# The last LayerNorm of a decoder layer: bias terms by adding DMAs, 1/sigma by ScalarE

## The chip, the cores and the metric

The kernel runs on one core of a Trainium2 chip. The core has five engines with an instruction stream each: TensorE (PE; its weight loads are listed as PEld), VectorE (DVE), ScalarE (ACT), GpSimd (POOL) and SyncE (SP), which in this kernel only issues DMAs. Data move between DRAM and the core's own memory (SBUF) by 16 DMA engines, and matmuls write into banks of PSUM. An engine executes its stream in order: an instruction that waits holds everything behind it on that engine. A DMA that is issued and waits for something holds its issuing engine in the same way.

The metric is the device time of one execution in microseconds, as the median of several runs. Lower is better.

## What is computed

One decoder layer over 4096 tokens of width 1024, in float32. Two mixers with a common input projection are followed by one output projection and a LayerNorm. What matters here is the end of it, from the reference:

```python
shift, scale, gate = jnp.split(mod, 3, axis=-1)
...
y = jnp.concatenate([y_a, y_b], axis=-1) @ w_out + b_out
x = layer_norm(DEEPNORM_ALPHA * x + gate[:, None, :] * y) * ln_post_g + ln_post_b
```

`gate` has one value per column (there is one sequence), so the gated bias `gate * b_out` is one row of 1024 values that is added to every token. DEEPNORM_ALPHA is 2 to the power 0.25. The LayerNorm needs the mean and the variance of each token, and 1/sigma = (variance + 1e-5) to the power -0.5.

## The kernel before

**Phases.** Phase 1 and phase 2 compute the input projection and what follows from it and leave their results in DRAM, by blocks of 512 tokens. The depthwise convolution and its LayerNorm run on VectorE beside them. Phase 3 takes the eight blocks of 512 tokens one after the other; it is the part that the change is in.

**A block of phase 3.** `prep(sb)` loads the convolution's results (`t`) and mixer A's results (`ya`), and splits each into a high part and a rest: matrices are multiplied as three products of such parts, so that TensorE's reduced precision loses little. The high part is a copy by ScalarE (L184), the rest a subtraction on VectorE (L185, in `split`). `pw_stage(sb)` does the pointwise product of the convolution branch: four results of 12 matmuls each, multiplied with `z` on VectorE, and split again into `yb0` to `yb3`. Then `out_tile(sb, t)` does four tiles of 128 tokens. Tiles are counted through all blocks, i = 4 sb + t, from 0 to 31.

**An output tile.** It loads 128 rows of x into a buffer `r` (L638; three buffers in turn) and forms ALPHA * x + gbo on VectorE (L639). `gbo` is the gated bias, the same row on all 128 partitions; it is made once in phase 1. TensorE multiplies the eight parts of y, 128 columns each (`ya` first, then `yb`), with the gated weights into two PSUM banks `po` of 512 columns: 48 matmuls (L647). There are four such banks, so two tiles can be under way. VectorE adds each bank to its half of `r` and sums the rows as it goes (L665, the eviction), and turns the sums into minus the mean (`osm`, L667). ScalarE squares `r` with that bias into a throwaway tile and sums it (L670, `oss`). VectorE turns this into variance plus epsilon (`ove`, L672), GpSimd raises it to -0.5 (`ors`, 1/sigma, L676). Two operations on VectorE finish the tile: (r - mean) * g (L678) and r * 1/sigma + b (L679), where `g_bc` and `b_bc` hold the rows of g and b on all partitions. SP stores `r` to `out` (L680). The very last tile, i = 31, computes its two halves one after the other and takes mean and variance from VectorE's own statistics operations.

**What else runs there.** Two of the eight blocks of the convolution are computed late, by VectorE, between the tiles (`late_unit`), and so is their LayerNorm (`conv_ln`). For that TensorE transposes the results into the bank `s2b`, ScalarE sums them, and GpSimd raises the variances to -0.5 (`ccs`, L263). TensorE then transposes the statistics (`ccp`).

**What sets the order.** The program is written as one sequence. A scheduler that simulates the engines with its own costs puts each engine's instructions into an order when the kernel is built; it follows data dependencies, free buffers and the dependencies that `after` adds by hand. SP issues nearly all loads and stores of phase 3 from one stream.

Of the kernel before, what the change touches and what calls it, by code (L numbers as in the profile page):

```python
# [9 lines left out]
F32 = mybir.dt.float32  # L10
# [3 lines left out]
ALU = mybir.AluOpType  # L14
# [3 lines left out]
P = 128  # L18
S = 4096
D = 1024  # L20
DH = 512
T = 512
NSB = S // T
TT = T // P
# [11 lines left out]
ALPHA = 2.0 ** 0.25  # L36
# [3 lines left out]
def tile_layer(ctx, tc, x, x_t, w_in_t, c, w_ada, b_ada, w_in, b_in, w_pool, b_pool, ls_pool, w_dw, b_dw,  # L40
# [20 lines left out]

# [1 line left out]
    ident = cst.tile([P, P], F32, name="ident")  # L63
# [28 lines left out]

# [1 line left out]
    crow = s2.tile([P, P], F32, tag="cto", bufs=2, name="crow", padded_shape=[P, T])  # L94
# [37 lines left out]

# [1 line left out]
    def mod_gate(acc):  # L134
# [48 lines left out]
    def split(hi, lo, src, eng=nc.vector):  # L183
        nc.scalar.copy(hi, src)  # L184
        eng.tensor_tensor(lo, src, hi.bitcast(F32), op=ALU.subtract)  # L185

# [48 lines left out]
    cD = [dr.tile([4 * TT, P], F32, name=f"cD{sb}") for sb in range(NSB)]  # L235
    rD = [dr.tile([8, P], F32, name=f"rD{sb}") for sb in range(NSB)]
    uD = [dr.tile([P, D], F32, name=f"uD{g}") for g in range(MC)]

# [3 lines left out]
    gate_bc = cst.tile([P, D], F32, tag="gate", name="gate_bc")  # L242
    gbo = cst.tile([P, D], F32, name="gbo")
    bpl = cst.tile([P, MC], F32, name="bpl")
    bu = cst.tile([P, MC], F32, name="bu")
    W = {}

# [1 line left out]
    ph_ctx = ExitStack()  # L249
# [116 lines left out]

    # modulation
    xt_next = [load_x(t) for t in range(TT)]
# [22 lines left out]
    for sb in range(NSB):  # L391
# [30 lines left out]
        if sb == 1:  # L422
            mod_gate(gbo)
            gb = wraw("gb")
            nc.sync.dma_start(gb, b_ada[2 * D : 3 * D].partition_broadcast(P))
            for h in range(2):
                sl = slice(h * 512, (h + 1) * 512)
                gp = tp_bank(f"gp{h}")
                nc.tensor.matmul(gp, ones, gbo[:, sl], start=True, stop=True)
                nc.vector.tensor_tensor(gate_bc[:, sl], gp, gb[:, sl], op=ALU.add)  # L430
            nc.sync.dma_start(gbo, b_out.partition_broadcast(P))
            nc.vector.tensor_tensor(gbo, gbo, gate_bc, op=ALU.mult)
    ph_ctx.close()
    lt = pool("lt", reuse_waits="tile")

# [1 line left out]
    ph_ctx = ExitStack()  # L437
# [52 lines left out]

# [1 line left out]
    def conv(m, s0, n, v, tmp, a):  # L492
# [94 lines left out]

# [1 line left out]
    ph = pool("ph3", reuse_waits="tile")  # L589
# [27 lines left out]
    def pw_stage(sb, vs, ys):  # L617
        for m in range(MC):
# [14 lines left out]
            ys.append(h2)  # L633

    def out_tile(sb, t, ys):
        i = sb * TT + t
        r = ph.tile([P, D], F32, tag="r", bufs=3, name=f"r{i}")
        nc.sync.dma_start(r, tok(xv, i))  # L638
        xg = nc.vector.scalar_tensor_tensor(r, r, ALPHA, gbo, op0=ALU.mult, op1=ALU.add)  # L639
        po = [acc_bank(f"po{i}_{h}") for h in range(2)]  # L640
        fin = i == NSB * TT - 1
        for hs in ((0,), (1,)) if fin else ((0, 1),):
            for k in range(KT):
                yh, yl = ys[k][:, 0, t * P : (t + 1) * P], ys[k][:, 1, t * P : (t + 1) * P]
                for lhs, wi, last in ((yh, 0, False), (yh, 1, False), (yl, 0, k == KT - 1)):
                    for h in hs:
                        mm = nc.tensor.matmul(po[h], lhs, Wo[k][wi][:, h * 512 : (h + 1) * 512],  # L647
                                              start=(k == 0 and wi == 0 and lhs is yh), stop=last)
                if k == 0 and hs[0] == 0:
                    after(xg, mm)  # L650
        halves = [slice(0, 512), slice(512, 1024)]
        if fin:
            bs = st.tile([P, 2, 6], F32, tag="xbs", bufs=4, name="obs")
            for h, sl in enumerate(halves):
                nc.vector.tensor_tensor(r[:, sl], po[h], r[:, sl], op=ALU.add)
                nc.vector.bn_stats(bs[:, h, :], r[:, sl])
# [5 lines left out]
        else:  # L662
            sm = st.tile([P, 3], F32, tag="osm", bufs=4, name=f"osm{i}")
            for h, sl in enumerate(halves):
                nc.vector.scalar_tensor_tensor(r[:, sl], po[h], 1.0, r[:, sl], op0=ALU.mult, op1=ALU.add,  # L665
                                               accum_out=sm[:, h : h + 1])
# [8 lines left out]
        rs = st.tile([P, 1], F32, tag="ors", bufs=4, name=f"ors{i}")  # L675
        nc.gpsimd.tensor_tensor(rs, ve, mhalf[:, 0:1], op=ALU.pow)  # L676
        for sl in halves:
            nc.vector.scalar_tensor_tensor(r[:, sl], r[:, sl], mean, g_bc[:, sl], op0=sub, op1=ALU.mult)  # L678
            nc.vector.scalar_tensor_tensor(r[:, sl], r[:, sl], rs, b_bc[:, sl], op0=ALU.mult, op1=ALU.add)  # L679
            nc.sync.dma_start(tok(ov, i)[:, sl], r[:, sl])  # L680
# [3 lines left out]
    for k in range(KT):  # L684
# [3 lines left out]
        hi, lo = wslot(f"wo{k}")  # L688
        split(hi, lo, raw)
        Wo.append((hi, lo))  # L690
    g_bc = cst.tile([P, D], F32, tag="gate", name="g_bc")
    nc.sync.dma_start(g_bc, ln_post_g.partition_broadcast(P))
    b_bc = ph.tile([P, D], F32, name="b_bc", bufs=1)
    nc.sync.dma_start(b_bc, ln_post_b.partition_broadcast(P))
# [45 lines left out]
```

## Time and profile before

| | |
|---|---|
| median of 3 runs | 1400.14 us (1399.49 to 1400.76) |
| span of the profiled execution | 1404.7 us (its time is not listed separately) |
| instructions in it | 17113 |
| ScalarE busy | 431.7 us (31%), 764 instructions |
| GpSimd busy | 167.2 us (12%), 203 instructions |
| DMA, mean over the span | 174 GB/s, 243.82 MB |
| queue of the DMAs that GpSimd issues | 33.56 MB, 7.2% of 16 engines' span |

The page has six parts: busy time by engine, the span in 40 slices (a digit is the busy share in tenths), the DMA queues, the chain of work that ended last, the costliest groups of instructions, and the DMA issues. A group's line names the source line, the engine, the operation, output and inputs by the program's names, the count, and then its busy time with the mean of one, and the idle time ahead of them with what ended most of it. The slices of 35.1 us show which phase a time falls in: phase 1 runs up to some 500 us, phase 2 from there to about 950 us, and the 32 output tiles lie between 957 and 1396 us, with a few microseconds at the end for the last tile's normalisation and store.

All transfers of GpSimd's queue are in phase 2 here (`x2r`, L326, which loads stored x-transposes): 64 of 512 KB. In phase 3 GpSimd has only the powers.

### The profile page before, as it was taken

The page shows a single profiled execution, that of the slowest core. Times are in us where ns is not written, and L with a number is a line of the kernel's source. Part 1 is how long each engine was busy: PE and PEld are TensorE (multiplying, and loading weights), DVE is VectorE, ACT ScalarE, POOL GpSimd, SP SyncE. Part 2 cuts the span into 40 slices and gives each one's busy share as a digit, 9 for nine tenths or more (in the row PEclk, how much of TensorE's full clock was granted, in tenths as well). Part 3 has the DMA queues.
Part 4 walks back from the last instruction along what each step waited for, and adds up shares of the span by engine and source line. Part 5 has one row for each costly group of instructions (what it writes and reads, how often), then busy time and mean ns, then how long its engine had stood idle before and what let it go on. Part 6 is the DMA issues. An engine that isn't in the chain of part 4 may idle for free.

```text
span 1404.7 us, 17113 instructions
## 1 busy us (share of the span) xinstructions
PE 1357.8 (97%) x6044; PEld 1118.6 (80%) x6044; DVE 1193.9 (85%) x2318; ACT 431.7 (31%) x764; POOL 167.2 (12%) x203
## 2 busy tenths in 40 slices
PE   3989999999999999999999999989999999999997
PEld 2878888888788888888888888778888888888886
DVE  7669999983479999899898699979897899998654
ACT  3535335344531322311114111434134131322310
POOL 4310000000100011110011110410111101001111
PEclk9999999999999999999999999989999999999999
DMA  9778776567474563361440741455444443433511
GB/s 313 235 279 312 257 276 241 173 255 242 162 253 151 174 210 124 111 202 42 161 166 31 239 136 61 136 183 173 161 173 138 155 158 122 157 128 122 191 62 75
DMA packets 119496, 243.82 MB, mean 174 GB/s; under 512 B 15026, under 2 KB 52722, under 8 KB 119410
## 3 DMA queue, kind: packets, MB, share of 16 engines
q1 hardware_dynamic: 109952, 209.07, 43.4%
q0 software_dynamic: 9216, 33.56, 7.2%
q8 instruction: 47, 0.77, 0.2%
q14 instruction: 39, 0.32, 0.1%
q10 hardware_dynamic: 242, 0.10, 0.0%
HBM read 156.65 MB, written 86.04 MB: 173 GB/s over the span
## 4 chain that ended last, share of the span: by engine, by line
PE 87%; DVE 4%; DMA 4%; ACT 2%; POOL 1%; issue 1%; SPq 1%; DVEq 0%; ACTq 0%
PE po L647 25%; PE p L335 6%; PE p L334 6%; PE p L333 6%; PE p2u L333 4%; PE p2u L334 4%; PE p2u L335 4%; PE p2z L333 4%; PE p2z L335 4%; PE p2z L334 4%; PE pw L623 2%; PE pw L625 2%; PE pw L624 2%; PE p2b L333 2%; PE p2b L335 2%; PE p2b L334 2%
## 5 line engine op out<-in xcount | busy, mean ns | idle before, releaser
L510 DVE SCALAR_TENSOR_TENSOR cx<-cv,wdw,cx 128x513 f32<-128x513 f32 (+1 forms) x240 | 144.6, 611 | 0.7
L510 DVE SCALAR_TENSOR_TENSOR ca<-cx,wsum,ca 128x256 f32<-128x256 f32 (+1 forms) x240 | 143.1, 608 | 0.1
L510 DVE SCALAR_TENSOR_TENSOR ca<-cv,wdw,ca 128x256 f32<-128x256 f32 (+1 forms) x224 | 133.5, 608 | 0.0
L676 POOL TENSOR_TENSOR ors<-ove,mhalf 128x1 f32<-128x1 f32 x32 | 46.3, 1447 | 409.3 <-DVE ove L672 400.9
L326 POOL DMA_DIRECT2D x2r<-xD x64 | 34.5, 540 | 402.7 <-PE p2b L335 276.4
L670 ACT ACTIVATE ojk<-r,osm 128x1024 bf16<-128x1024 f32 x31 | 35.6, 1149 | 148.3 <-DVE osm L667 148.3
L665 DVE SCALAR_TENSOR_TENSOR r<-po,r 128x512 f32<-128x512 f32 x62 | 40.8, 685 | 23.3 <-PE po L647 23.3
L510 DVE SCALAR_TENSOR_TENSOR lx<-lv,wdw,lx 128x257 f32<-128x257 f32 x120 | 57.2, 477 | 0.0
L510 DVE SCALAR_TENSOR_TENSOR la<-lx,wsum,la 128x256 f32<-128x256 f32 x120 | 57.0, 475 | 0.0
L451 ACT ACTIVATE sz<-p2z,cols 128x512 f32<-128x512 f32 x32 | 22.0, 687 | 108.0 <-PE p2z L335 108.0
L263 POOL TENSOR_TENSOR xcs<-smx,mhalf 128x1 f32<-128x1 f32 x28 | 19.2, 688 | 290.7 <-DVE smx L262 263.9
L297 ACT ACTIVATE x<-xk,shc 128x512 fp32r<-128x512 f32 x56 | 38.5, 721 | 47.5 <-DVE xk L288 46.1
L510 DVE SCALAR_TENSOR_TENSOR la<-lv,wdw,la 128x256 f32<-128x256 f32 x112 | 52.9, 475 | 0.0
L286 DVE TENSOR_TENSOR xk<-xk,xbc 128x1024 f32<-128x1024 f32 x28 | 34.0, 1220 | 16.7 <-DMA xk<-in_x_t_dram 16.5
L263 POOL TENSOR_TENSOR ccs<-smc,mhalf 128x1 f32<-128x1 f32 x32 | 37.2, 1169 | 91.9 <-DVE smc L262 91.2
L298 DVE SCALAR_TENSOR_TENSOR x<-xk,shc,x 128x512 fp32r<-128x512 f32 x56 | 40.4, 744 | 8.1 <-ACT x L297 8.1
L458 ACT ACTIVATE u<-p2u,bu 128x512 f32<-128x512 f32 x32 | 22.0, 689 | 75.6 <-PE p2u L335 75.6
L679 DVE SCALAR_TENSOR_TENSOR r<-r,ors,b_bc 128x1024 f32<-128x1024 f32 (+1 forms) x33 | 41.0, 1246 | 3.2 <-POOL ors L676 3.1
L647 PE MATMUL po<-wo0h,ya 128*128 128x512 f32 x128 | 41.2, 392 | 0.0
L647 PE MATMUL po<-wo1h,ya 128*128 128x512 f32 x128 | 41.1, 390 | 0.0
L259 ACT ACTIVATE x<-x 128x1024 f32<-128x1024 f32 x28 | 29.6, 1059 | 35.7 <-DMA x<-in_x_dram 35.2
L639 DVE SCALAR_TENSOR_TENSOR r<-r,gbo 128x1024 f32<-128x1024 f32 x32 | 38.9, 1217 | 1.8 <-DMA r<-in_x_dram 1.8
(356 smaller groups left out, 4137.8 us busy)
## 6 DMA issues: line engine op xcount, KB each, us to landing
x2r<-xD POOLq DMA_DIRECT2D x64, 512.0 KB, 7.8
xD<-x SPq DMA_DIRECT2D x56, 512.0 KB, 6.9
x<-in_x_dram SPq DMA_DIRECT2D x32, 512.0 KB, 7.9
r<-in_x_dram SPq DMA_DIRECT2D x32, 512.0 KB, 4.4
out_dram<-r SPq DMA_DIRECT2D x31, 512.0 KB, 2.6
xk<-in_x_t_dram SPq DMA_DIRECT2D x28, 512.0 KB, 6.5
wa<-in_w_ada_dram SPq DMA_DIRECT2D x32, 256.0 KB, 4.8
wr<-in_w_in_dram SPq DMA_DIRECT2D x16, 512.0 KB, 6.5
```

The costliest lines, as they stand in the source:

```text
L263: nc.gpsimd.tensor_tensor(rstd, sm[:, 2:3], mhalf[:, 0:1], op=ALU.pow)
L297: nc.scalar.activation(h2[:, 0, :], z, AF.Identity, bias=shc[:, k : k + 1])
L298: nc.vector.scalar_tensor_tensor(h2[:, 1, :], z, shc[:, k : k + 1], h2[:, 0, :].bitcast(F32), op0=ALU.add, op1=ALU.subtract)
L333: nc.tensor.matmul(ps, wh, X[0], start=first, stop=False)
L334: nc.tensor.matmul(ps, wh, X[1], start=False, stop=False)
L335: nc.tensor.matmul(ps, wl, X[0], start=False, stop=last)
L510: nc.vector.scalar_tensor_tensor(dst, src, wt, dst, op0=ALU.mult, op1=ALU.add)
L639: xg = nc.vector.scalar_tensor_tensor(r, r, ALPHA, gbo, op0=ALU.mult, op1=ALU.add)
L647: mm = nc.tensor.matmul(po[h], lhs, Wo[k][wi][:, h * 512 : (h + 1) * 512], start=(k == 0 and wi == 0 and lhs is yh), stop=last)
L665: nc.vector.scalar_tensor_tensor(r[:, sl], po[h], 1.0, r[:, sl], op0=ALU.mult, op1=ALU.add, accum_out=sm[:, h : h + 1])
L676: nc.gpsimd.tensor_tensor(rs, ve, mhalf[:, 0:1], op=ALU.pow)
L679: nc.vector.scalar_tensor_tensor(r[:, sl], r[:, sl], rs, b_bc[:, sl], op0=ALU.mult, op1=ALU.add)
```

## The change

It changes five things, all for the 31 tiles ahead of the last but where it says otherwise.

1. **The gated bias.** `gbo` becomes b_out * gate / ALPHA (one operation on VectorE as before), and its first row is stored to a small DRAM buffer `gD`. The SBUF buffer is then reused for `b_bc`, which is loaded in phase 1 now.
2. **Loading r.** SP loads x into `r` as before, and a second DMA, issued by GpSimd, adds the row `gD` to all 128 partitions of `r` in place. L639 is gone. This holds for all 32 tiles. The eviction computes r * ALPHA + po (the same operation on VectorE with other operands); in the last tile it takes the place of an addition. There are four buffers of `r` in the place of three.
3. **The final bias.** Ahead of each load of `r`, SP stores `b_bc` to the rows of `out` that belong to the tile (the fill). It waits for a marked operation of VectorE: the multiplication by g of the tile three before, or a split of the weights for the first ones.
4. **1/sigma.** ScalarE multiplies `r` by it (L685 of the changed kernel), in the place of L679 on VectorE, which also added b.
5. **The store.** GpSimd issues a DMA that adds `r` to the filled rows of `out`. The last tile keeps its two operations on VectorE and its plain stores.

```diff
+    gD = dr.tile([1, D], F32, name="gD")
...
-    gbo = cst.tile([P, D], F32, name="gbo")
+    gbo = cst.tile([P, D], F32, tag="gbo", name="gbo")
...
-            nc.vector.tensor_tensor(gbo, gbo, gate_bc, op=ALU.mult)
+            nc.vector.scalar_tensor_tensor(gbo, gbo, 1.0 / ALPHA, gate_bc, op0=ALU.mult, op1=ALU.mult)
+            nc.sync.dma_start(gD, gbo[0:1, :])
...
+    def load_r(i):
+        r = ph.tile([P, D], F32, tag="r", bufs=4, name=f"r{i}")
+        if i < NSB * TT - 1:
+            after(nc.sync.dma_start(tok(ov, i), b_bc), marks[-min(len(marks), 3)], True)
+        nc.sync.dma_start(r, tok(xv, i))
+        nc.gpsimd.dma_start(r, gD[0].partition_broadcast(P), accum_op=ALU.add)
+        return r
...
-        r = ph.tile([P, D], F32, tag="r", bufs=3, name=f"r{i}")
-        nc.sync.dma_start(r, tok(xv, i))
-        xg = nc.vector.scalar_tensor_tensor(r, r, ALPHA, gbo, op0=ALU.mult, op1=ALU.add)
+        r = load_r(i)
...
-                nc.vector.scalar_tensor_tensor(r[:, sl], po[h], 1.0, r[:, sl], op0=ALU.mult, op1=ALU.add,
+                nc.vector.scalar_tensor_tensor(r[:, sl], r[:, sl], ALPHA, po[h], op0=ALU.mult, op1=ALU.add,
                                                accum_out=sm[:, h : h + 1])
...
+        if not fin:
+            marks.append(nc.vector.scalar_tensor_tensor(r, r, mean, g_bc, op0=sub, op1=ALU.mult))
+            nc.scalar.mul(r, r, rs)
+            nc.gpsimd.dma_start(tok(ov, i), r, accum_op=ALU.add)
+            return
...
-        split(hi, lo, raw)
+        marks = [split(hi, lo, raw)]
...
-    b_bc = ph.tile([P, D], F32, name="b_bc", bufs=1)
+    b_bc = cst.tile([P, D], F32, tag="gbo", name="b_bc")
```

The change also moves instructions on the engines. Line numbers in the rows below are those of each kernel's own text; a number behind the last underscore of a name only tells buffers apart.

GpSimd, in the block of tiles 20 to 23. Before, five powers of tiles 19 to 23 stand one behind the other:

```order
L676 TENSOR_TENSOR ors19_10106<-ove19_10104,mhalf_82 128x1
L676 TENSOR_TENSOR ors20_10342<-ove20_10340,mhalf_82 128x1
L676 TENSOR_TENSOR ors21_10409<-ove21_10407,mhalf_82 128x1
L676 TENSOR_TENSOR ors22_10476<-ove22_10474,mhalf_82 128x1
L676 TENSOR_TENSOR ors23_10543<-ove23_10541,mhalf_82 128x1
```

In the changed kernel the powers are at L682, the adding stores at L686 and the adding loads at L642:

```order
L682 TENSOR_TENSOR ors20_10365<-ove20_10363,mhalf_82 128x1
L686 DMA out_0_dram<-r20_10302 128x1024
L642 DMA r24_10808<-gD_317 128x1024
L682 TENSOR_TENSOR ors21_10433<-ove21_10431,mhalf_82 128x1
L686 DMA out_0_dram<-r21_10370 128x1024
L642 DMA r25_10876<-gD_317 128x1024
L682 TENSOR_TENSOR ors22_10501<-ove22_10499,mhalf_82 128x1
L686 DMA out_0_dram<-r22_10438 128x1024
L642 DMA r26_10944<-gD_317 128x1024
```

Between the powers of two tiles there are now the adding store of the one and the adding load of the tile four later, whose buffer `r` is the one that the store reads.

ScalarE, at the end of the block of tiles 16 to 19. `ojk18` and `ojk19` are the squares of the last two tiles, `yb5_0` to `yb5_3` the high parts of the pointwise product that tiles 20 to 23 need, `vp6` those of a product one block later. Before:

```order
L670 ACTIVATE ojk18_10034,oss18_10035<-r18_9977,osm18_10030 128x1024
L184 CAST yb5_0_10184<-z5_0_10181 128x512
L184 CAST yb5_1_10201<-z5_0_10181 128x512
L670 ACTIVATE ojk19_10101,oss19_10102<-r19_10044,osm19_10097 128x1024
L184 CAST vp6_2_10255<-t6_2_10252 128x512
L184 CAST vp6_3_10261<-t6_3_10258 128x512
L184 CAST yb5_2_10220<-z5_2_10217 128x512
L184 CAST yb5_3_10237<-z5_2_10217 128x512
```

After, with the scalings at L685:

```order
L676 ACTIVATE ojk18_10055,oss18_10056<-r18_9997,osm18_10051 128x1024
L685 ACTIVATE r18_9997<-r18_9997,ors18_10060 128x1024
L676 ACTIVATE ojk19_10123,oss19_10124<-r19_10065,osm19_10119 128x1024
L184 CAST yb5_0_10206<-z5_0_10203 128x512
L685 ACTIVATE r19_10065<-r19_10065,ors19_10128 128x1024
L184 CAST yb5_1_10223<-z5_0_10203 128x512
L184 CAST vp6_2_10277<-t6_2_10274 128x512
L184 CAST yb5_2_10242<-z5_2_10239 128x512
L184 CAST vp6_3_10283<-t6_3_10280 128x512
L184 CAST yb5_3_10259<-z5_2_10239 128x512
```

The scaling of tile 18 stands between the two squares, and that of tile 19 between the copies for `yb5_0` and `yb5_1`.

SP, near the end. Before, loads of `r` (L638) and stores to `out` (L680) alternate:

```order
L638 DMA r28_11122<-in_x_dram 128x1024
L680 DMA out_0_dram<-r26_10916 128x1024
L638 DMA r29_11189<-in_x_dram 128x1024
L680 DMA out_0_dram<-r27_10983 128x1024
L638 DMA r30_11256<-in_x_dram 128x1024
L680 DMA out_0_dram<-r28_11122 128x1024
L638 DMA r31_11323<-in_x_dram 128x1024
```

After, `t7` are the loads of `prep` for the last block (L605), L640 the fills from `b_bc`, L641 the loads of `r`:

```order
L605 DMA t7_1_10774<-tD1_7_252 128x512
L545 DMA tD3_7_268<-la7_2_10133 128x512
L640 DMA out_0_dram<-b_bc_7919 128x1024
L605 DMA t7_2_10780<-tD2_7_260 128x512
L605 DMA t7_3_10786<-tD3_7_268 128x512
L641 DMA r28_11152<-in_x_dram 128x1024
L640 DMA out_0_dram<-b_bc_7919 128x1024
L641 DMA r29_11220<-in_x_dram 128x1024
L640 DMA out_0_dram<-b_bc_7919 128x1024
L641 DMA r30_11288<-in_x_dram 128x1024
```

The stores of `r` are gone from SP's stream, and in their place each load of `r` has a fill ahead of it; loads of the next block's `t` stand behind the fill that waits for VectorE.

More of the change, by code (lines that the diff above doesn't have):

```diff
@@ L184, in split @@
         nc.scalar.copy(hi, src)
-        eng.tensor_tensor(lo, src, hi.bitcast(F32), op=ALU.subtract)
+        return eng.tensor_tensor(lo, src, hi.bitcast(F32), op=ALU.subtract)
     def wslot(name):
@@ L646, in out_tile @@
                     for h in hs:
-                        mm = nc.tensor.matmul(po[h], lhs, Wo[k][wi][:, h * 512 : (h + 1) * 512],
+                        nc.tensor.matmul(po[h], lhs, Wo[k][wi][:, h * 512 : (h + 1) * 512],
                                               start=(k == 0 and wi == 0 and lhs is yh), stop=last)
-                if k == 0 and hs[0] == 0:
-                    after(xg, mm)
         halves = [slice(0, 512), slice(512, 1024)]
@@ L654, in out_tile @@
             for h, sl in enumerate(halves):
-                nc.vector.tensor_tensor(r[:, sl], po[h], r[:, sl], op=ALU.add)
+                nc.vector.scalar_tensor_tensor(r[:, sl], r[:, sl], ALPHA, po[h], op0=ALU.mult, op1=ALU.add)
                 nc.vector.bn_stats(bs[:, h, :], r[:, sl])
```

## The prediction

> **What bounds the kernel now.** The page's first two parts come first: which engine is busy, and whether it is so everywhere.
>
> ```profile
> span 1404.7 us, 17113 instructions
> PE 1357.8 (97%) x6044; PEld 1118.6 (80%) x6044; DVE 1193.9 (85%) x2318; ACT 431.7 (31%) x764; POOL 167.2 (12%) x203
> PE   3989999999999999999999999989999999999997
> ```
>
> TensorE is busy for 97% of the span, and every slice but the first, the last and two others is full. VectorE's 85% is high, but it is no bound unless TensorE waits for it. So the next view is the busy time by stretch, cut where the stages change (columns: stretch, its length, busy time and count of PE, PEld, DVE, ACT, POOL, then PE's clock, DMA share, GB/s).
>
> ```profile
> 900.00:957.00 57.00, 49.75 (x211) 40.56 (x210) 49.17 (x91) 21.09 (x36) 12.66 (x3) 0.91 0.50 162
> 957.00:1396.00 439.00, 439.00 (x1945) 361.75 (x1944) 369.81 (x742) 119.81 (x212) 49.78 (x39) 1.00 0.41 141
> 1396.00:1405.00 9.00, 0.87 (x4) 0.38 (x2) 4.39 (x8) 0.00 (x0) 0.92 (x1) 0.75 0.15 58
> ```
>
> The changed stage, the 32 output tiles, is the middle row. There TensorE is busy 439.00 of 439.00 us at full clock: work taken from any other engine in it has nothing to shorten. The stage can only stay, or grow a wait. The list of TensorE's waits has one large entry outside the start-up:
>
> ```profile
> PE ccp L77 <- POOL ccs L263: 7.3, 1, 7.3
> ```
>
> **The change part by part.** The profile's own time is not listed beside its span; the span is 1404.7 us, 4.6 above the median 1400.14 of the runs. I work with differences inside the span and add them to that median.
>
> What goes from VectorE:
>
> ```profile
> L679 DVE SCALAR_TENSOR_TENSOR r<-r,ors,b_bc 128x1024 f32<-128x1024 f32 (+1 forms) x33 | 41.0, 1246 | 3.2 <-POOL ors L676 3.1
> L639 DVE SCALAR_TENSOR_TENSOR r<-r,gbo 128x1024 f32<-128x1024 f32 x32 | 38.9, 1217 | 1.8 <-DMA r<-in_x_dram 1.8
> L670 ACT ACTIVATE ojk<-r,osm 128x1024 bf16<-128x1024 f32 x31 | 35.6, 1149 | 148.3 <-DVE osm L667 148.3
> L676 POOL TENSOR_TENSOR ors<-ove,mhalf 128x1 f32<-128x1 f32 x32 | 46.3, 1447 | 409.3 <-DVE ove L672 400.9
> L326 POOL DMA_DIRECT2D x2r<-xD x64 | 34.5, 540 | 402.7 <-PE p2b L335 276.4
> L185 DVE TENSOR_TENSOR yb<-z,yb 128x512 fp32r<-128x512 f32 x32 | 21.9, 684 | 4.4 <-ACT yb L184 4.4
> ```
>
> All 32 of L639 (38.9) and 31 of the 33 of L679 (31 x 1.27 = 39.4) leave VectorE: 78 us, 2.5 a tile. By the stage's row TensorE gains none of it. The eviction (now r times ALPHA plus po) keeps its form and its 0.69 us. ScalarE gets 31 scalings of 128x1024; the nearest row is L670 at 1.15 us, 36 us in all, on an engine that is busy 119.81 of 439 us. The changed product for gbo, its store to gD and the earlier load of b_bc lie in phase 1, alone and beside full slices: nothing, while TensorE stays full there. If they moved work there, at most one 1.27 us operation is late.
>
> What is added is 31 stores of b_bc, 32 adding loads and 31 adding stores of 512 KB, the adding ones issued by GpSimd. For the price of a transfer, from issue to landing, I read the DMA issues of the stretch 1100 to 1390, and of the whole run, and the queue's bytes and share:
>
> ```profile
> r<-in_x_dram SPq DMA_DIRECT2D x21, 512.0 KB, 3.6
> out_dram<-r SPq DMA_DIRECT2D x21, 512.0 KB, 2.6
> ...
> x2r<-xD POOLq DMA_DIRECT2D x64, 512.0 KB, 7.8
> r<-in_x_dram SPq DMA_DIRECT2D x32, 512.0 KB, 4.4
> q1 hardware_dynamic: 109952, 209.07, 43.4%
> ```
>
> 209.07 MB in 43.4% of 1404.7 us is 343 GB/s, so 512 KB keep the 16 engines 1.53 us. Per tile the fill adds 1.5, the adding load 1.5 to 3.1 and the adding store 0 to 1.5: 3 to 6 us in 13.6, which lifts the DMA share of 0.41 to between 0.63 and 0.86. Room remains, but transfers wait for each other more. I therefore take the whole run's 4.4 us for a load of r and not the 3.6 of this stretch.
>
> An adding store is in no row. Its bounds: 2.6 us, if adding is free, and 7.8 + 3.6 = 11.4, the slowest row of GpSimd's queue (eight issued together) plus a load. I take 6.2, a load of what is added to (3.6) and then the store (2.6), since the sum can't be written before its old part is read.
>
> The Trainium skill, "Collectives: The Full Stack", section on the bandwidth ceiling, says that adding in a transfer costs no cycles but a second read, and measures a factor of 1.93. By it an adding store would take an estimated 2.6 + 0.93 x 1.53 = 4.0 us, and the sum below would come to no loss; no row of this trace has such a transfer.
>
> The order of GpSimd and ScalarE (shown with the change) decides what this costs. In the middle of a block of four tiles GpSimd has: adding store of r21, adding load of r25, power for tile 22. The load into r25 reuses r21's buffer, so it starts once the store has landed; the adding load waits for it, and behind that, in order, stands the power of tile 22, which its scaling on ScalarE needs, and so its store. That is a **closed cycle**, once a tile: power 1.45, scaling 1.15, adding store S, load 4.4, issue of the adding load 0.54, and five handoffs. One handoff:
>
> ```profile
> 1377.85 0.15 DVE L672 TENSOR_SCALAR ove<-oss 128x1 f32<-128x1 f32 x1 [1.37 <-ACT ojk L670]
> ...
> 1378.14 1.46 POOL L676 TENSOR_TENSOR ors<-ove,mhalf 128x1 f32<-128x1 f32 x1 [9.42 <-DVE ove L672]
> ```
>
> 1378.14 - 1378.00 = 0.14, five times 0.7. So the cycle is 8.2 + S: 14.4 us with S = 6.2. TensorE's pace is in the chain of waits:
>
> ```profile
> 1211.63 21.78 PE po L647 x96
> ```
>
> 96 matmuls are two tiles: 0.227 each, 10.9 us a tile; with 48 more for the pointwise product a block of four takes 54.5. Three such cycles fall into most blocks (P20 to P23), so the last power of a block comes 3 x (14.4 - 10.9) = 10.6 us later than TensorE's pace wants it.
>
> Who waits: on ScalarE the scaling of tile 19 now stands ahead of the casts yb5_1 to yb5_3, which TensorE needs for the second half of tile 20. Cover: tile 19 ended at 1211.63 + 21.78 = 1233.4, and its power began 7.2 us later:
>
> ```profile
> 1240.61 1.46 POOL L676 TENSOR_TENSOR ors<-ove,mhalf 128x1 f32<-128x1 f32 x1 [9.38 <-DVE ove L672]
> 1302.71 0.61 ACT L184 CAST yb<-z 128x512 fp32r<-128x512 f32 x1
> ```
>
> Power 1.45, scaling 1.15, cast 0.61, VectorE's subtraction 0.68 and four handoffs 0.6 bring yb5_1 to 11.7 us after the tile's end. In the changed order 78 matmuls, 17.7 us, stand between that end and the first one that reads it. So 6.0 us of lag are covered, and 10.6 - 6.0 = 4.6 aren't. Of the eight blocks the first starts with four free buffers and the last has no next one: 6 seams x 4.6 = 28 us. The mean pace says the same: four cycles of 14.4 are 57.6 against 54.5, 3.1 a block, 25 in eight. I take 26: **1426 us**.
>
> Cheaper edits with one answer: a fill of out waits for the multiplication by g of the tile three before, and behind it on SP stands the next load of r and then ya, z and t for the next block. That multiplication no longer waits for anything of GpSimd, so a fill is late only when VectorE is; it costs nothing while the adding store decides the load's start, and up to one r load (4.4 us) a block if it decides instead. The fourth buffer of r makes the wait one tile longer than three would. The tail keeps its path: the last tile is evicted, normalised and stored as before, and tile 30's adding store, some 8 us after that tile's end, has the last 11 us to land.
>
> **Rivals.** First, adding is nearly free: S = 2.6 and a load of 3.6 give 7.4 + 2.6 = 10.0, under the 10.9 of a tile. No lag builds up, TensorE stays full, and the time is **1400**. The low DMA share speaks for it; that a sum needs a second read speaks against it.
>
> Second, it gets faster. TensorE's 7.3 us wait at ccp comes from one power on GpSimd, by the rows of tile ccs (min, median, max in ns):
>
> ```profile
> L263 POOL TENSOR_TENSOR ccs<-smc,mhalf x4: 542/2616/12020, 894.9 to 916.9; 128x1 f32<-128x1 f32 x4
> ```
>
> One of four took 12.02 us, while VectorE ran two-source operations without a gap from 904.8 to 916.5; it ended when VectorE ran dry. If the regrouped VectorE rows there leave a gap early, with adding free, the wait goes: **1393**. Against it: the changed order has 22 rows there before VectorE must wait, where 21 stood.
>
> Third, the same starving spreads. Before, L679 on VectorE waited for the power and so made room for it within 0.5 us; now no multiplication or addition on VectorE waits for it. If powers took 3 us longer in this stage, three cycles add 9 us to each seam, 54 in six: **1480**. It decides once VectorE runs gapless for over about 2 us at a power; in this stage the powers took 1.45 on average in spite of 84% busy, which speaks against it. The Trainium skill, "SBUF — State Buffer", section on who interferes with whom, says that a VectorE instruction with two SBUF inputs contends with a GpSimd one that reads SBUF; the 12.02 us agree with it.
>
> Fourth, the transfers choke: S = 9.6, midway between 7.8 and 11.4, gives a cycle of 17.8, a lag of 20.8, and (20.8 - 6.0) x 6 = 89 us: **1489**.
>
> **How the numbers follow.** The closed cycle with a moderate price 0.5, adding free 0.2, faster 0.1, starving 0.1, choking 0.1. The likeliest is the first. Slower by over 0.2% (2.8 us, about what a measurement of this kernel tells from no change) is 0.7, within it 0.2, faster 0.1. The range reaches from the faster case to the choking one, 1394 to 1488. The likeliest case alone, S from 5 to 7.8, spans 1405 to 1455.
>
> **What would show it.** Right: on TensorE new waits in the stage at the second half of a block's first tile or at ccp, led back to ScalarE and GpSimd; GpSimd held by a DMA ahead of powers; adding stores of about 6 us. Wrong: a full TensorE row from 957 on (adding is free), powers that are long by themselves (starving), or waits at the eviction for r (the adding loads are the slow ones, not the stores).

## The result, and the profile after

| | before | after |
|---|---|---|
| median | 1400.76 us (1399.49 to 1411.42, 5 runs) | 1464.86 us (1462.43 to 1477.70, 5 runs) |
| ratio to before, 95% interval | 1 | 1.0451 (1.0410 to 1.0493) |
| span of the first profiled execution | 1404.7 us | 1475.9 us (its time: 1477.70 us) |
| tail stage in it | 442.2 us | 511.3 us |

The change makes the kernel 64 us slower. The forecast was 26 us slower, with a range up to 1488 us.

The tail stage is measured here from the first pointwise matmul to the statistics of the last tile's second half. By that measure the first traces show 69.1 us more. Two lines of the page first, the engines and the slices:

```profile
PE 1382.4 (94%) x6044; PEld 1132.3 (77%) x6044; DVE 1123.0 (76%) x2255; ACT 464.2 (31%) x795; POOL 211.2 (14%) x266
PE   3989999999999999999999997999969899987987
```

Behind the start-up the row of TensorE is full up to 1070 us but for one slice (886 to 922 us, ahead of the stage, a wait at `ccp` like the one before the change). From 1070 us on, the end of the stage's second block, it is broken. VectorE is 71 us lighter, and nobody gained by it. Busy time by stretch, the stage alone, before and then after (columns as in the prediction):

```profile
955.40:1397.60 442.20, 441.47 (x1955) 363.41 (x1953) 371.38 (x745) 121.19 (x214) 49.78 (x39) 1.00 0.41 140
```

```profile
957.50:1468.80 511.30, 465.49 (x1955) 375.67 (x1954) 299.91 (x682) 153.53 (x244) 92.40 (x102) 0.95 0.72 185
```

The same 1955 matmuls. TensorE is idle for 511.30 - 465.49 = 45.8 us, and *busy* for 24.0 us longer, at a granted clock of 0.95 (465.49 x 0.95 = 442, about the busy time before). Its waits in that stretch (in total, how many, the longest):

```profile
PE po L655 <- ACT yb L184: 11.2, 8, 2.5
PE cl L77 <- ACT cl L262: 11.1, 2, 7.8
PE ccp L77 <- POOL ccs L264: 9.0, 2, 5.0
PE po L655 <- DVE r L671: 7.7, 3, 6.4
PE pw L625 <- DVE z L632: 6.1, 2, 3.5
```

They add up to 45.1 us. Only the first is the one that the prediction priced, the high parts of the pointwise product. Traced back, the larger ones lead to one place, the load of r that waits for the adding store. On GpSimd the adding load waits for it, ahead of powers:

```profile
POOL r L642 <- DMA r<-in_x_dram: 219.5, 27, 11.7
POOL ors L682 <- DVE ove L678: 108.0, 15, 19.7
```

The adding load (L642) held GpSimd 27 times, up to 11.7 us each, for the load of r under it. On SP, whose stream has other loads behind the load of r, the load's wait for the store has grown to the longest in total; whole trace, before and then after:

```profile
SPq L638 <- DMA out_dram<-r: 58.1, 27, 4.2
```

```profile
SPq L641 <- DMA out_dram<-r: 251.2, 28, 14.7
```

The chain of work that ended last shows one round of it, from a power to the next:

```profile
1328.87 0.90 POOL ors L682
1329.77 0.02 issue
1329.79 1.16 ACT r L685
1330.95 0.40 issue
1331.35 5.35 DMA out_dram<-r
...
1336.76 5.13 DMA r<-in_x_dram
...
1341.96 0.59 issue
1342.55 0.04 POOL r L642
1342.59 0.54 issue
1343.12 0.88 POOL ors L682
```

Power, scaling, adding store, load of r, adding load, next power: 1343.12 - 1328.87 = 14.25 us. That is the closed cycle of the prediction, at nearly the length that it had there (14.4). The powers of tiles 20 and 23 start at 1315.09 and 1356.72 us: three rounds take 41.6 us, 13.9 each.

One victim, traced to its cause on ScalarE. First the waits on that engine, then TensorE's:

```profile
1066.44 0.19 ACT L676 ACTIVATION_READ_ACCUMULATOR ojk<-r,osm 128x1 f32 x1
1079.85 1.15 ACT L685 ACTIVATE r<-r,ors 128x1024 f32<-128x1024 f32 x1 [13.22 <-POOL ors L682]
1080.91 0.58 ACT L260 ACTIVATE cl<-cl 128x512 f32<-128x512 f32 x1
```

```profile
1082.92 0.90 PE L77 MATMUL cl<-ident,la 128*128 128x128 f32 x3 [7.83 <-ACT cl L262]
```

The scaling waited 13.22 us for a late power; behind it stood the convolution's statistics `cl`, whose bank TensorE needed for the next transposes.

### The profile page after: what moved, and what is told of

Its sections match the earlier page's. It is cut to its first block, busy times and chain, and to the rows that moved or that the text cites. A ratio compares the mean times of both kernels' runs of the same rounds, so it can differ in the third digit from the quotient of the medians.

```text
span 1475.9 us, 17243 instructions
## 1 busy us (share of the span) xinstructions
PE 1382.4 (94%) x6044; PEld 1132.3 (77%) x6044; DVE 1123.0 (76%) x2255; ACT 464.2 (31%) x795; POOL 211.2 (14%) x266
## 5 line engine op out<-in xcount | busy, mean ns | idle before, releaser
L512 DVE SCALAR_TENSOR_TENSOR cx<-cv,wdw,cx 128x257 f32<-128x257 f32 (+1 forms) x240 | 145.7, 615 | 0.6
L685 ACT ACTIVATE r<-r,ors 128x1024 f32<-128x1024 f32 x31 | 35.6, 1150 | 155.3 <-POOL ors L682 155.3
L642 POOL DMA_DIRECT2D r<-gD x32 | 28.0, 874 | 305.9 <-DMA r<-in_x_dram 219.5
L185 DVE TENSOR_TENSOR yb<-z,yb 128x512 fp32r<-128x512 f32 x32 | 21.9, 687 | 53.3 <-ACT yb L184 53.2
L671 DVE SCALAR_TENSOR_TENSOR r<-r,po 128x512 f32<-128x512 f32 x62 | 40.5, 683 | 28.2 <-PE po L655 27.7
L682 POOL TENSOR_TENSOR ors<-ove,mhalf 128x1 f32<-128x1 f32 x32 | 38.5, 1204 | 113.9 <-DVE ove L678 108.0
L655 PE MATMUL po<-wo0h,ya 128*128 128x512 f32 x128 | 44.5, 422 | 7.7 <-DVE r L671 7.7
L185 DVE TENSOR_TENSOR ya<-ya,ya 128x512 fp32r<-128x512 f32 x32 | 21.1, 688 | 33.0 <-ACT ya L184 33.0
L655 PE MATMUL po<-wo6h,yb 128*128 128x512 f32 x128 | 41.5, 403 | 4.0 <-ACT yb L184 4.0
```

Source lines behind the costliest of these rows:

```text
L185: return eng.tensor_tensor(lo, src, hi.bitcast(F32), op=ALU.subtract)
L512: nc.vector.scalar_tensor_tensor(dst, src, wt, dst, op0=ALU.mult, op1=ALU.add)
L642: nc.gpsimd.dma_start(r, gD[0].partition_broadcast(P), accum_op=ALU.add)
L671: nc.vector.scalar_tensor_tensor(r[:, sl], r[:, sl], ALPHA, po[h], op0=ALU.mult, op1=ALU.add, accum_out=sm[:, h : h + 1])
L685: nc.scalar.mul(r, r, rs)
```

## The experiments

All ran beside the kernel before on the same chip; ratios have their 95% interval. The kernel before had a median of 1400.1 to 1400.8 us beside most runs and of 1408.96 beside e5 to e8, so the ratios are what to compare. "Stage" is the tail stage of the run's trace (one trace each), "waits" TensorE's listed waits in it, "growth" the stage less 442.2 us.

| run | median us | ratio to before | stage us | waits us | growth / waits |
|---|---|---|---|---|---|
| changed kernel | 1464.86 | 1.0451 (1.0410 to 1.0493) | 511.3 | 45.1 | 1.53 |
| e1 adding load later | 1417.63 | 1.0126 (1.0079 to 1.0172) | 462.8 | 14.2 | 1.45 |
| e2 plain store | 1420.91 | 1.0126 (1.0081 to 1.0172) | 468.4 | 17.3 | 1.51 |
| e3 early fills | 1489.98 | 1.0599 (1.0536 to 1.0662) | 504.6 | 44.7 | 1.40 |
| e4 no adding store | 1404.63 | 1.0025 (1.0000 to 1.0051) | 446.6 | 3.4 | 1.29 |
| e5 later, early fills | 1448.09 | 1.0308 (1.0152 to 1.0464) | 466.0 | 16.9 | 1.41 |
| e6 later, plain store | 1412.16 | 1.0022 (0.9980 to 1.0064) | 452.7 | 7.8 | 1.35 |
| e7 no adding load | 1414.00 | 1.0045 (1.0011 to 1.0079) | 449.2 | 4.6 | 1.52 |
| e8 made wait | 1409.35 | 1.0012 (0.9970 to 1.0054) | 443.4 | 0.8 | |
| e9 plain load of the row | 1459.08 | 1.0411 (1.0372 to 1.0451) | 503.5 | 42.3 | 1.45 |
| e10 e4, adding load later | 1403.21 | 1.0012 (0.9991 to 1.0033) | 453.0 | 5.9 | 1.83 |
| e11 before again | 1401.16 | 1.0002 (0.9967 to 1.0038) | 442.3 | 0.0 | |
| e12 changed kernel again | 1469.06 | 1.0457 (1.0367 to 1.0546) | 516.7 | 51.0 | 1.46 |

**e1: the adding load later in GpSimd's order.**

```diff
-        nc.gpsimd.dma_start(r, gD[0].partition_broadcast(P), accum_op=ALU.add)
+        ad = nc.gpsimd.dma_start(r, gD[0].partition_broadcast(P), accum_op=ALU.add)
+        if i >= 2:
+            after(ad, pows[i - 2])
...
-        nc.gpsimd.tensor_tensor(rs, ve, mhalf[:, 0:1], op=ALU.pow)
+        pows.append(nc.gpsimd.tensor_tensor(rs, ve, mhalf[:, 0:1], op=ALU.pow))
```

> The same transfers as in the changed kernel; only GpSimd's order differs: the adding load of tile i stands behind the power of tile i-2 (P22, A24, S22 where it was S20, A24, P21). Theory 'closed cycle' (power, scaling, adding store, load of r, adding load, next power, 13.1 to 14.2 us in the changed kernel's trace against 10.9 us of TensorE a tile): the load of r now has two tiles, 21.8 us, for its 13, so no power waits for it, TensorE's waits in the tail stage fall from 45 us to under 10, and the time is 1400 to 1415 us. Theory 'transfers choke' (stage's DMA share 0.41 before, 0.52 to 0.80 now): nothing is taken away, 1450 to 1470 us. Theory 'fills' (the fill waits for VectorE and holds the loads behind it on SP): 1450 to 1470 us.

Measured: 1417.63 us, the stage 462.8. With the same transfers, 48.5 of the 69.1 us of the stage are gone. GpSimd's timeline, tiles 20 and 21:

```profile
1270.86 1.53 POOL L684 TENSOR_TENSOR ors<-ove,mhalf 128x1 f32<-128x1 f32 x1 [19.12 <-DVE ove L680]
1272.36 0.88 POOL L642 DMA_DIRECT2D r<-gD  x1
1273.99 0.85 POOL L688 DMA_DIRECT2D out_dram<-r  x1 [0.76 <-ACT r L687]
1276.56 1.53 POOL L684 TENSOR_TENSOR ors<-ove,mhalf 128x1 f32<-128x1 f32 x1 [1.72 <-DVE ove L680]
```

Nearly all adding loads find their data there by then, and each power waits for its own tile (`ove`) alone. The edit names GpSimd only, but the scheduler also moved some of the late convolution's operations on VectorE; e2 below leaves the orders as they were but for single operations. Choking transfers as the main cause fall: the DMA share is higher than in the changed kernel (0.79 against 0.72 in the stage) and adding stores take longer, 9.4 us in the median, and yet most of the loss is gone. The size fell short of the expectation: 14.2 us of waits, not under 10, and 1417.63 us, 2.6 above its upper end.

**e2: a plain store in its place.**

```diff
-            nc.gpsimd.dma_start(tok(ov, i), r, accum_op=ALU.add)
+            nc.gpsimd.dma_start(tok(ov, i), r)
```

> The store of r is a plain one on GpSimd's queue instead of an adding one; the final bias is left out of the output of 31 tiles by that. The order and the number of transfers stay. Theory 'closed cycle': with a store of 3.0 us (2.6 in the kernel before) in the place of 5.6 the cycle is 10.5 to 11.6 us, about TensorE's 10.9 a tile: 1400 to 1425 us. Theory 'transfers choke', by their number and bytes written: most of the loss stays, 1440 us or more. Theory 'fills': unchanged, 1450 to 1470 us.

Measured: 1420.91 us. The stores land sooner (min, median, max, of the changed kernel and of e2):

```profile
DMA to landing us min/median/max: 5.0/5.6/12.2
```

```profile
DMA to landing us min/median/max: 2.9/3.8/12.7
```

Adding costs 1.8 us in the median, 2.1 in the fastest. The cycle is 14.25 - 1.8 = 12.4 us then (in e2's trace the powers of tiles 20 and 23 are 36.0 us apart, 12.0 a round), and the stage is 42.9 us shorter: a small part of the cycle makes most of the loss, since only what goes beyond a threshold is paid (the working of it stands in the next section).

**e3: the fills don't wait.**

```diff
-            after(nc.sync.dma_start(tok(ov, i), b_bc), marks[-min(len(marks), 3)], True)
+            nc.sync.dma_start(tok(ov, i), b_bc)
```

> The fills of out no longer wait for a multiplication of VectorE; all else as in the changed kernel. Theory 'fills': loads behind them on SP come early, 1400 to 1430 us. Theory 'closed cycle': the load of r still waits for the adding store, and the adding load for it, 1455 to 1475 us. Theory 'transfers choke': 1455 us or more.

Measured: 1489.98 us, 15 above the range that the closed cycle gave. All 31 fills were now issued in phase 1 (200.8 to 245.8 us of the trace), and the stage began at 976.0 us, where it began at 957.5 in the changed kernel. The stage itself, without one fill in it, is 504.6 us. It is 6.7 us shorter than that of the changed kernel's first trace, and two traces of that kernel differ by 5.4 us. So the fills and their wait aren't the cause; taken out of the stage in this way they cost more ahead of it than they give in it.

**e4: the adding store undone.**

```diff
-            after(nc.sync.dma_start(tok(ov, i), b_bc), marks[-min(len(marks), 3)], True)
...
-            nc.scalar.mul(r, r, rs)
-            nc.gpsimd.dma_start(tok(ov, i), r, accum_op=ALU.add)
+            nc.vector.scalar_tensor_tensor(r, r, rs, b_bc, op0=ALU.mult, op1=ALU.add)
+            nc.sync.dma_start(tok(ov, i), r)
```

> The adding store, the fills and ScalarE's scaling are undone (VectorE multiplies by 1/sigma and adds the final bias, SP stores plainly); the adding load and four buffers of r stay, and the adding load stays ahead of the next power on GpSimd. Theory 'closed cycle': power 0.9, VectorE 1.25, store 2.6, load of r 3.6 to 4.4, issue 1.1 and handoffs 0.6 make 10.1 to 10.9 us, just under TensorE's 10.9: 1400 to 1412 us. Theory 'transfers choke': two of three added transfers are gone, about a third of the loss stays, 1415 to 1425 us. If the adding loads alone are slow (5.6 us to landing), waits of TensorE at the eviction for r and 1420 us or more.

Measured: 1404.63 us, the stage 4.4 us longer than before, as expected of a closed cycle of 10 to 11 us. The adding loads stand ahead of the powers as before; with a plain store by SP behind VectorE the round is short enough.

**e5 and e6: what is left in e1.** Both keep its order; e5 adds e3's edit, e6 that of e2.

> As in e1 (adding load of tile i behind the power of tile i-2), and the fills of out don't wait, so that they are all issued in phase 1 and none is left in the tail stage. Measured by the stage's length, from the first pointwise matmul to the last tile's statistics: 442 us in the kernel before, 511 in the changed one, 463 in e1, 505 with early fills alone. Theory 'what is left in e1 is transfer time' (stores of 9.4 us, DMA share 0.81, the late convolution's loads behind fills and loads of r on SP): without 31 fills the share falls to about 0.65, the stores to about 5.5 us, and the stage to 445 to 455 us. Theory 'what is left in e1 is ScalarE's scalings ahead of the copies': 460 to 466 us. The whole time is longer than the stage tells, since early fills cost about 20 us ahead of the stage in e3.

> As in e1, with a plain store of r in the place of the adding one; the final bias is left out of 31 tiles by that. Theory 'transfer time': an adding store moves 1.5 us more of the 16 engines a tile, DMA share about 0.70; the stage falls from e1's 463 to 446 to 455 us. Theory 'scalings ahead of the copies': 460 to 466 us.

Measured: e5's stage is 466.0 us, as the theory of the scalings had it, and no shorter than e1's 462.8, so the fills' traffic isn't what is left. e6's is 452.7, as the theory of transfer time had it, and 10.1 shorter. So about half of e1's growth of 20.6 us is the price of adding. What stands behind the rest can be read in e1's trace: its three longest waits of TensorE (5.78, 3.47 and 2.81 us, 12.1 of 14.2) each follow a load on SP that came late. VectorE waited 6.35 and 4.62 us for `lv`, inputs of the late convolution (1.6 at most in the kernel before), and ScalarE 10.04 us for `t`. The longest, on VectorE and, behind VectorE's multiplication with `z`, on TensorE:

```profile
1130.17 0.35 DVE L510 TENSOR_SCALAR la<-lv,wdw 128x256 f32<-128x256 f32 x1 [6.35 <-DMA lv<-vD]
```

```profile
1134.76 0.80 PE L625 MATMUL pw<-vp,wpw0h 128*128 128x512 f32 x1 [5.78 <-DVE z L632]
```

So most of what TensorE still waits for in e1 has late loads behind it. How much of their lateness is slow transfers, the adding ones among them, and how much is their place behind loads of r on SP was not separated. The scalings are at most a part of the 7.0 us of e7 below.

**e7: no adding load.**

```diff
-        nc.gpsimd.dma_start(r, gD[0].partition_broadcast(P), accum_op=ALU.add)
```

> The adding load is left out, and with it the gated bias of the output; adding stores, fills and scalings stay as in the changed kernel. The closed cycle is open by that, since no GpSimd instruction waits for a load of r any more. Theory 'closed cycle': the stage is 445 to 460 us (511 in the changed kernel), not above e1's 463, which has the adding loads on top. Theory 'adding stores are what costs': their 5.6 us stay, 490 us or more.

Measured: the stage is 449.2 us. Adding stores, fills, scalings ahead of the casts: together they cost 7.0 us when nothing on GpSimd waits for a load. 62 of the 69 us of the stage hang on that one line.

**e8: a made wait.** Ahead of `split` for `yb1` in five blocks:

```diff
+            if m == 1 and 0 < sb < 6:
+                for _ in range(16):
+                    slow = nc.scalar.activation(z, z, AF.Identity)
```

> The kernel before with 16 copies of z in place (0.69 us each) on ScalarE ahead of the cast of yb1 in five blocks: a made wait of TensorE of some us, five times, and nothing else changed. Theory 'a wait costs more than its length, since TensorE's granted clock is about half for some 5 us after it': the stage grows by 1.4 to 1.6 times the sum of TensorE's waits that the profile lists in it, and the rows after each wait show a clock of 0.5 to 0.6. Theory 'a wait costs its length': 1.0 to 1.1 times.

Inconclusive: the scheduler knew of the copies and put other work on TensorE meanwhile (its order in the stage differs from that of the kernel before); only 0.8 us of wait came of them. What a wait costs is read from the table instead: in eleven stages with 3.4 to 51.0 us of waits the growth is 1.29 to 1.83 times the waits, in nine of them 1.35 to 1.53.

**e9: the adding load replaced by a plain one**, at its place.

```diff
-        nc.gpsimd.dma_start(r, gD[0].partition_broadcast(P), accum_op=ALU.add)
+        nc.gpsimd.dma_start(r, gD[0].partition_broadcast(P))
```

> The adding load is replaced by a plain load of the same row at the same place of GpSimd's stream; x is left out of the output by that. It still waits for the load of x into r, since it writes the same buffer. Theory 'closed cycle': what counts is that a DMA which waits for that load stands ahead of the next power, not that it adds (its own landing is not in the cycle); the stage stays at 495 to 515 us (511 in the changed kernel, 442 in the kernel before). Theory 'the adding of the load is what costs': 445 to 465 us.

Measured: 1459.08 us, the stage 503.5. So it isn't the adding of the load, it is its place and what it waits for.

**e10: e4 with e1's order.**

> Of the change only the adding load, the product for gbo and the fourth buffer of r are left, and the adding load of tile i stands behind the power of tile i-2; VectorE does the last two operations of a tile and SP stores plainly, as in the kernel before. Theory 'closed cycle': in e4, the same with the adding load ahead of the next power, the cycle of 10.1 to 10.9 us left 4.4 us in the stage; with the new place the stage is 442 to 444 us, and 1396 to 1402 us in all (if TensorE's wait of 7.3 us at ccp ahead of the stage stays away as in e4, some 8 us below what the stage tells). Theory 'transfers choke': the adding loads remain, the stage stays at 446 us or more.

Measured: 1403.21 us, 1.2 above the range of the closed cycle, but within the measurement of the kernel before (1.0012, 0.9991 to 1.0033). Its trace was of its longest execution (1418.21 us) and shows a stage of 453.0 us, not the 442 to 444 expected: by the stage, the theory that transfers choke (446 us or more) came out. Its two waits of TensorE, 3.49 and 2.43 us, follow late loads as in e1: VectorE waited 7.61 us for `lv`, ScalarE 8.13 us for `t`. So late loads look like a second, smaller cost of the added transfers; it is one trace that shows it here. No version here beats the kernel before.

**e11 and e12: both kernels a second time**, for another trace of each.

> The kernel before, unchanged, for a second trace of the same program. Theory 'the wait of 7.3 us at ccp ahead of the tail stage happens in some executions only, by how GpSimd's power and VectorE's operations fall in time': the times fall into two groups some 10 us apart (7.3 us and the lower clock behind it), and this trace either shows no such wait, a power of under 3 us there and a time near 1400 us, or shows it again at 1405 to 1413 us. Theory 'it belongs to the program': the wait is there at 1400 us too. In both the tail stage is 442 us without a wait.

> The changed kernel, unchanged, for a second trace; the first is of an execution of 1477.7 us with a median of 1464.9. Theory 'the difference is the wait at ccp ahead of the stage (8.2 us and the clock behind it)': in an execution near 1464 us that wait is missing, and the tail stage is 505 to 515 us, as in the first trace. Theory 'the tail stage itself varies': the wait is there and the stage is about 498 us.

Measured: e11's trace is of an execution of 1398.63 us, its span is 1396.9, and the wait at `ccp` isn't there. The rows of GpSimd's four powers ahead of it (min, median, max in ns), first that of e11, with the same program as the row in the prediction:

```profile
L263 POOL TENSOR_TENSOR ccs<-smc,mhalf x4: 734/1045/1921, 896.7 to 908.6; 128x1 f32<-128x1 f32 x4
```

and that of the changed kernel's first trace:

```profile
L264 POOL TENSOR_TENSOR ccs<-smc,mhalf x4: 543/2612/12400, 896.3 to 918.6; 128x1 f32<-128x1 f32 x4
```

So that wait comes and goes between executions of one program; with it the stage starts 955.4 - 947.5 = 7.9 us later. In e12's trace (1471.56 us) it is missing too, and the stage is 516.7 us, which neither theory had: the stage itself varies by some 5 us. Without that wait on either side, 1471.56 - 1398.63 = 72.9 us stand against 516.7 - 442.3 = 74.4 us of stage. The loss is all in the tail stage.

## Why the prediction was right in its way and wrong in its size

**The bound.** Right: the 78 us taken from VectorE bought nothing, since TensorE had no wait in the stage that VectorE ended. (VectorE's sum fell by 71 only: its other operations took some 1% longer in that trace, one of the convolution's 751 ns against 743.)

**The cycle.** Right in its parts and its length: S was taken as 6.2 us and is 5.6 in the median, the load of r as 4.4 and is 5.13 in the quoted round, the cycle as 14.4 and that round is 14.25. e1, e2, e7 and e9 show that it is the cause: move the waiting instruction back in the order, and 48.5 us of the stage go; make one link 1.8 us shorter, and 42.9 go; take the waiting instruction out, and 62 go; leave it there and only stop it from adding, and 8 go.

**"So the last power of a block comes 3 x (14.4 - 10.9) = 10.6 us later than TensorE's pace wants it."** Here is the first term that was too small. The pace of 10.9 us a tile is not that of the evictions in a block: the first two tiles are worked on in turns and end together. Rows of the kernel before, VectorE's second eviction of tiles 20, 21 and 23:

```profile
1260.09 0.68 DVE L665 SCALAR_TENSOR_TENSOR r<-po,r 128x512 f32<-128x512 f32 x1
...
1264.62 0.68 DVE L665 SCALAR_TENSOR_TENSOR r<-po,r 128x512 f32<-128x512 f32 x1
```

```profile
1287.61 0.69 DVE L665 SCALAR_TENSOR_TENSOR r<-po,r 128x512 f32<-128x512 f32 x1
```

Three intervals take 27.5 us, not 32.7; with it the prediction's own cycle gives 3 x 14.4 - 27.5 = 15.7. In the changed kernel the last tile of a block, tile 23 here, has its second eviction and its power at

```profile
1337.41 0.68 DVE L671 SCALAR_TENSOR_TENSOR r<-r,po 128x512 f32<-128x512 f32 x1
```

```profile
1356.72 0.83 POOL L682 TENSOR_TENSOR ors<-ove,mhalf 128x1 f32<-128x1 f32 x1
```

19.3 us apart. In the six middle blocks these distances are 23.6, 17.0, 11.0, 8.6, 19.3 and 20.3 us, against 2.6 in the undisturbed tile 30: a lag of 14.0 us on average where 10.6 was forecast.

**"So 6.0 us of lag are covered, and 10.6 - 6.0 = 4.6 aren't."** As a sum the cover holds: the six lags less 2.6 and less 6.0 each add up to 48 us, and TensorE's waits are 45.1. Seam by seam it holds in part: the uncovered lags are 15.0, 8.4, 2.4, 0.0, 10.7 and 11.7 us, the waits in the block behind each 14.3, 8.2, 3.5, 6.4, 8.3 and 4.4, so at the fourth and the last the agreement of the sum is luck. The same working gives e2, with its cycle of 12.4 us, 3 x 12.4 - 27.5 - 6.0 = 3.7 us a seam, 22 in six, where 17.3 were listed, and e4, with 10.1 to 10.9, nothing, where 3.4 were; for the changed kernel with its 14.25 it gives 9.3 a seam, 55 in six. So where a lag builds up it comes out somewhat too high. That these waits are all at the second half of a block's first tile doesn't hold. ScalarE's scaling stands ahead of the convolution's statistics too (11.1 us at `cl`), and TensorE's next wait at `ccp` (9.0) has the same behind it: the last powers there waited for VectorE's `smc`, which is made from these statistics.

```profile
1361.91 1.20 POOL L264 TENSOR_TENSOR ccs<-smc,mhalf 128x1 f32<-128x1 f32 x2 [1.88 <-DVE smc L263]
```

And on SP the load of r, which waits for the adding store, stands ahead of `ya` and `t`; 10.5 of the 45.1 us came that way (6.43, 2.51 and 1.51). This was told of for the fill and not for the load. The longest wait of this sort, at the fourth seam, on ScalarE and then on TensorE:

```profile
1310.01 1.14 ACT L184 CAST ya<-ya 128x512 fp32r<-128x512 f32 x2 [11.39 <-DMA ya<-yD]
```

```profile
1312.62 1.40 PE L655 MATMUL po<-wo0h,ya 128*128 128x512 f32 x2 [6.43 <-DVE r L671]
```

The cast waited 11.39 us for `ya`, whose load stood behind a load of r on SP; VectorE's half of the split waited for the cast, and behind it the eviction that TensorE needed a bank from.

**"6 seams x 4.6 = 28 us."** Here is the second term that was too small: a wait was priced at its length. Behind it TensorE runs at a lower clock. The stretches ahead of the end of that 6.43 us wait, just after it, and after that:

```profile
1300.00:1312.60 12.60, 6.19 (x28) 4.79 (x26) 1.94 (x5) 1.14 (x2) 0.85 (x1) 0.92 0.74 192
1312.60:1318.00 5.40, 5.38 (x14) 4.05 (x15) 3.56 (x10) 2.59 (x4) 1.53 (x1) 0.56 0.65 212
1318.00:1330.00 12.00, 12.00 (x54) 9.94 (x53) 2.87 (x7) 1.20 (x3) 2.36 (x3) 1.00 0.58 145
```

14 matmuls in 5.4 us, where 24 would fit at full clock. The Trainium skill, "TensorE: Matmul & The Clock Gate", in its part on the clock gate, says that an idle window of about 3.4 us halves the array's clock until a busy one has passed; that agrees with these rows. But waits shorter than the window cost clock here too. These are the stretches behind one of 2.51 us, which ended at 1108.36:

```profile
1108.30:1110.40 2.10, 2.04 (x6) 1.66 (x7) 2.06 (x4) 2.10 (x6) 0.00 (x0) 0.70 1.06 211
1110.40:1113.00 2.60, 2.60 (x8) 2.02 (x7) 1.13 (x2) 1.14 (x3) 0.00 (x0) 0.59 0.75 279
1113.00:1117.00 4.00, 4.00 (x19) 3.31 (x18) 1.90 (x4) 1.59 (x3) 0.00 (x0) 1.00 0.95 265
```

Cut into steps of 1 us from the end of a wait, the granted clock is 0.50 for five whole steps behind the waits of 7.83 and 5.03 us, for three behind one of 3.45, and stays at 1.00 behind one of 1.51. So the price of a wait is not in proportion to its length; one and a half times is what comes out over the waits of these stages.

So the steps of the prediction that failed are two terms of its sum. The lag of a block's last power was put at 10.6 us and was 14.0; with waiters that it had not counted, 28 us of waits became 45.1. And the price of a wait was put at its length and was 1.53 times that, by the clock: 69.1 us. The prediction's own view had the second: its row for 900 to 957 us has a clock of 0.91 beside the 7.3 us wait at `ccp`.

**The rivals.** *Adding is nearly free* falls for the changed kernel; e2, whose store adds nothing, is still 1.0126 (1.0081 to 1.0172). *Faster, without the wait at ccp*: that wait does vanish in some executions, but those of the kernel before as well, so it is no gain of the change. *Starving*: the changed kernel's 32 powers of the last LayerNorm took 1.20 us on average, below the 1.45 of before; it falls. *Choking* falls as the main cause by e1; as a part it is seen in e6, 10 us of what e1 has left, and in the late loads of e1 and e10. The Trainium skill, "Collectives: The Full Stack", in the section on the bandwidth ceiling, has the second read as the price of adding; the fastest landing of 5.0 us against 2.9 goes that way; the estimate of 4.0 us that the prediction worked out from it was too low by 1.0 for the fastest store and by 1.6 for the median.

**Edits costed at nothing.** The changed product for gbo, the earlier load and the tail show nothing: without the long power the stage starts at 946.0 us in the changed kernel (e12) and at 947.5 before (e11), and 7.1 us follow the stage in both first traces. That the fills cost nothing while the store decides is not tested closely: e3's stage without them is 6.7 us shorter, about what two traces of one kernel differ by.

## What to carry to other kernels

Before work is moved to an engine that looks idle, write down what stands behind each waiting instruction in that engine's stream, DMAs it issues included: here one DMA issue that waited for a buffer, ahead of a 1.2 us operation, cost 62 us, and moving it two tiles back in the stream gave 48.5 back. Compare a cycle with the pace of the tiles as they end, not with their mean, and price a wait of TensorE of some 2.5 us and more above its length, since the clock falls behind it; in this kernel it came to about one and a half times. Time taken from an engine that nobody waits for is worth nothing, however much it is.

## What the runs showed of the hardware that was not expected

- TensorE's clock is granted at half for 3 to 6 us behind the waits of 2.5 us and more that are named above, and stays full behind one of 1.51 us (rows and steps above).
- One 128x1 power on GpSimd took 12.02 us in one execution and at most 1.92 us in another of the same program, among the same gapless VectorE operations; most times of the kernel before lie at 1396 to 1403 us or at 1407 to 1414. e11's trace, without the long power, is of 1398.63 us; the first, with it, of about 1406.4 (its span and the 1.7 us that e11 has around its own). That the power makes the two groups is argued from that, not shown.
- An adding DMA store of 512 KB lands in 5.0 us at best, a plain one on the same queue in 2.9, and in e1, where it runs beside more transfers, in 9.4 in the median.
